# Feed-forward: both parts of an activation in one 512-column product, the down projection in two passes

## Chip, cores and metric

The kernel runs on one core of a Trainium2 chip. The metric is the device time of one execution in microseconds: 1619.3 us, the median of three runs from 1618.78 to 1620.37.

## What is computed

A transformer block with attention, a gated recurrence and 16 experts is followed by a second block of two layers. Each of these layers is a feed-forward, a mixer, and a second feed-forward, on 256 tokens of width 1024. The change touches the four feed-forwards (width 2816) and, in the layout of the activations only, every projection:

```python
def swiglu(x, w_gate, w_up, w_down):
    return (jax.nn.silu(x @ w_gate) * (x @ w_up)) @ w_down

for l in range(DEPTH_2):
    h = x + 0.5 * swiglu(rms_norm_2(x, ffn1_norm[l]), ffn1_gate[l], ffn1_up[l], ffn1_down[l])
    ...
    x = h + 0.5 * swiglu(rms_norm_2(h, ffn2_norm[l]), ffn2_gate[l], ffn2_up[l], ffn2_down[l])
return rms_norm_2(x, final_norm)
```

Everything is float32.

## The kernel before

Activations lie with features on partitions and the 256 tokens along the row; a matrix of 1024 features is eight chunks of 128. A float32 product is made of float32r ones: weights and activations are each split in a high part (a rounded copy, by ScalarE) and a low part (what is left, by VectorE). `mm3` (L409) multiplies low weights by high activations, high by low and high by high, three products of 256 columns into one region of PSUM, each with a weight load of its own.

Weights come in slots of 1 MB ([128, 2048]) through four raw buffers, in a fixed order (`stream`); `pump` fetches when a raw buffer is free. `cut` (L331) splits half a slot: ScalarE writes 128x1024 of `wh` (L333), VectorE the same of `wl` (L334). A split slot takes two of the 17 ring buffers of 8 KB; x, the norm's two parts and the mixer's large tiles live in the same ring. `ahead(i)` (L343) splits slot i and up to `la` further ones while the ring has room beyond `hold`, with a priority that lies `late` instructions behind. A scheduler orders each engine's instructions by priority as their operands become ready; on the chip each engine then runs its queue in that order. Splits traced after a norm's reciprocal root are kept behind it on VectorE (`gate`).

PSUM has eight banks: a pool of four (`pa`), one of three (`pb`) and one alone (`pc`).

A feed-forward (`ffn`, L1241) has 22 steps j. A gate/up slot holds 128 gate and 128 up columns; `proj` (L578) makes their 48 products into one bank, gate in one half and up in the other. `evac` (L1247) multiplies by the norm's row (VectorE, 512 columns), takes Silu of the gate (ScalarE), multiplies by up (VectorE) and splits the result in `hh` (ScalarE) and `hl` (VectorE). `down` (L1260) multiplies them with half a down slot, 24 products over all eight output chunks, which accumulate in the four banks of `pa` over all 22 steps, two chunks in a bank. Step j's down products come two steps later.

`start_phase` (L502) begins a phase: for each of eight chunks the residual's update from PSUM (VectorE, `adder`), the split of x times the norm's weight (ScalarE and VectorE), its square, and the products of the first three slots with this chunk. In the last chunk the sum of squares goes through TensorE (`fin1`), then come the reciprocal root on VectorE and its transposition (`fin2`), in the middle of the next projection. The first feed-forward starts beside the last expert with one slot (`first_phase`). After the last feed-forward the final norm runs with no weights left to multiply.

Of the kernel before, what the change touches and what calls it, by code (L numbers as in the profile page):

```python
# [140 lines left out]
def _prepare(i):  # L141
# [14 lines left out]
    for l in range(2):  # L156
        for n in ("ffn1", "ffn2"):
            ga, up = _pairs(f[n + "_gate_2"][l], st), _pairs(f[n + "_up_2"][l], st)
            out[f"{n}gu{l}"] = np.stack([ga, up], axis=3).reshape(NF, 128, 2048)
            out[f"{n}d{l}"] = _rows(f[n + "_down_2"][l])  # L160
# [49 lines left out]
# ---------------------------------------------------------------- the kernel  # L210
# [11 lines left out]
def _body(tc, nc, const, ringp, work, psum, a, out):  # L222
    V, S, PE, G = nc.vector, nc.scalar, nc.tensor, nc.gpsimd

    # ------------------------------------------------------------ memory
    st = {"ring": 0, "raw": 0, "next": 0, "hold": 0, "la": 2, "late": 0, "gate": None}
# [11 lines left out]
    def later(n):  # L238
        """as if traced n instructions further on"""
# [37 lines left out]
    # the first slot of block 2 is split while the last one of the experts is on its way  # L277
# [86 lines left out]
    def keep_warm(n, w, x, late=5000):  # L364
        """n products that nobody reads, for gaps in which TensorE's clock would fall back"""
# [5 lines left out]
    # ------------------------------------------------------------ constants  # L371
# [37 lines left out]
    def mm3(ps, wh, wl, xh, xl, first, last):  # L409
        PE.matmul(ps, lhsT=wl, rhs=xh, start=first, stop=False, skip_group_check=True)  # L410
        PE.matmul(ps, lhsT=wh, rhs=xl, start=False, stop=False, skip_group_check=True)  # L411
        PE.matmul(ps, lhsT=wh, rhs=xh, start=False, stop=last, skip_group_check=True)  # L412

    def behind(i, j):
        """i is issued after j, both on one engine"""
# [3 lines left out]
    def hilo(hi, lo, src):  # L419
        """src (SBUF or PSUM) in two float32r parts"""  # L420
# [3 lines left out]
    class Norm:  # L424
        """x * g in parts, and 1/rms of x: by tokens on partitions (rt) and along rows (rb)."""

        def __init__(self, g, parts=True, late=0):
# [3 lines left out]
            if parts:  # L431
                self.xh = ralloc([128, 8, 256], F32R, "xh")
                self.xl = ralloc([128, 8, 256], F32R, "xl")
# [3 lines left out]
        def split(self, c):  # L437
                xc = xt[:, c]
                g = self.g[:, c:c + 1]
                h = S.activation(self.xh[:, c], xc, AF.Copy, scale=g)  # L440
                l = V.scalar_tensor_tensor(self.xl[:, c], xc, g, self.xh[:, c].bitcast(F32),
                                       op0=OP.mult, op1=OP.subtract)
# [7 lines left out]
        def square(self, c, add=True):  # L450
            """add: into the sum; else left to TensorE"""
# [20 lines left out]
        def fin2(self, rev=False, bank=pc):  # L472
            """rev: also the rows with each 128 tokens back to front (rr)"""
# [16 lines left out]
    def wpair(i):  # L490
        """slot of two output chunks -> (hi, lo) by (chunk, contraction chunk)"""
# [4 lines left out]
    def warm(func):  # L496
        """the table of func, ahead of its use"""
# [3 lines left out]
    def start_phase(norm, update, jobs, each=None, bank=None, func=None):  # L501
        """Chunk by chunk: the residual's update, its parts, and the first products.  # L502
        jobs: (output, weights by chunk, first of its bank, last of its bank)"""
        for c in range(8):
# [6 lines left out]
            for n, (ps, w, first, last) in enumerate(jobs):  # L511
# [3 lines left out]
                mm3(ps, wh, wl, norm.xh[:, c], norm.xl[:, c], c == 0 and first, c == 7 and last)  # L515

    def ordered(*seq):
        """issued in this order, all on one engine"""
# [3 lines left out]
    def first_phase(norm, update, i, ps, each):  # L522
        """start_phase for one slot, step by step beside the last expert"""
# [34 lines left out]
        for c in range(8):  # L558
            each(c)
            for m in range(2):  # L560
                if c == 7 and m:
                    norm.fin1(pa)
                mm3(ps[:, m], wh[:, m, c], wl[:, m, c], norm.xh[:, c], norm.xl[:, c],
                    c == 0 and m == 0, c == 7 and m == 1)
# [10 lines left out]
    def proj(norm, i, ps, mid=None):  # L575
        ahead(i)
        wh, wl = wpair(i)
        for m in range(2):  # L578
            for c in range(8):
                mm3(ps[:, m], wh[:, m, c], wl[:, m, c], norm.xh[:, c], norm.xl[:, c], c == 0, c == 7)  # L580
# [4 lines left out]
    def proj_t(norm, i, ps, mid=None):  # L585
        """512 output columns with tokens on partitions; ps: a bank for each 128 tokens"""
        for s in range(2):
# [4 lines left out]
            for t in range(2):  # L592
                for k in range(4):
                    c = 4 * s + k
                    xh, xl = (x[:, c, 128 * t:128 * t + 128] for x in (norm.xh, norm.xl))
# [8 lines left out]
    def out_proj(slots, order, mh, ml, each=None):  # L604
        """contraction chunks in the order of the slots, all 8 output chunks at a time"""
        acc = [pa(f"acc{b}") for b in range(4)]
        for n, i in enumerate(slots):
# [3 lines left out]
            def mul(m, o):  # L611
                k = order[2 * n + m]
                f, z = n == 0 and m == 0, n == len(slots) - 1 and m == 1
                mm3(acc[o // 2][:, o % 2], wh[:, m, o], wl[:, m, o], mh[:, k], ml[:, k],
# [23 lines left out]

    def run(gen, n=1):
# [5 lines left out]
    # ================================================================ block 1  # L645
# [31 lines left out]
    # lower bounds of the forget gates: softmax over the two rows, the first of them  # L677
# [24 lines left out]
    def gates(p, d, h):  # L702
        """heads h, h + 1 of direction d: f -> T0, k -> AL (forward) or AR (backward)"""
# [39 lines left out]
    def hgrn():  # L743
        """A[s, t] of every head: what each token t takes of each token s, level by level"""
# [821 lines left out]
```

## Time and profile before

| | |
|---|---|
| median of three runs | 1619.3 us (1618.78, 1619.3, 1620.37) |
| span of the profiled execution, first to last instruction | 1618.6 us; no other time is listed for it |
| instructions | 28848 |
| TensorE, VectorE, ScalarE busy | 1504.8, 821.7, 609.5 us |
| read from memory | 397.99 MB |

The page gives each engine's busy time, the span in 40 slices, the DMA queues, and a chain of waits followed back from the last instruction. From 0 to about 190 us the first mixer runs, then the experts, whose weights are read as they are, to about 640 us, and then the second block. PE is TensorE's products, PEld its weight loads, DVE VectorE, ACT ScalarE. A product's listed duration reaches from its start to the end of its results, so consecutive ones overlap; the distance between two starts is the pace.

### The profile page before, as it was taken

The page shows a single profiled execution, that of the slowest core. Times are in us where ns is not written, and L with a number is a line of the kernel's source. Part 1 is how long each engine was busy: PE and PEld are TensorE (multiplying, and loading weights), DVE is VectorE, ACT ScalarE, POOL GpSimd, SP SyncE. Part 2 cuts the span into 40 slices and gives each one's busy share as a digit, 9 for nine tenths or more (in the row PEclk, how much of TensorE's full clock was granted, in tenths as well). Part 3 has the DMA queues.
Part 4 walks back from the last instruction along what each step waited for, and adds up shares of the span by engine and source line. Part 5 has one row for each costly group of instructions (what it writes and reads, how often), then busy time and mean ns, then how long its engine had stood idle before and what let it go on. Part 6 is the DMA issues. An engine that isn't in the chain of part 4 may idle for free.

```text
span 1618.6 us, 28848 instructions
## 1 busy us (share of the span) xinstructions
PE 1504.8 (93%) x12440; PEld 1265.0 (78%) x12440; DVE 821.7 (51%) x1472; ACT 609.5 (38%) x992; POOL 6.1 (0%) x11
## 2 busy tenths in 40 slices
PE   9999988777686779999999999999999999999998
PEld 9887633222232236999999999999999999999997
DVE  7975412000000003955548866655755648866653
ACT  6445201000000002644446655444443437655432
POOL 0000000000000000000000000000000000000000
PEclk9999999777878769999999999999999999999999
DMA  7546799999999998855433637453555433637520
GB/s 298 187 153 240 305 403 421 421 420 421 421 421 421 421 422 347 294 204 186 176 124 107 254 117 292 161 204 131 208 208 184 159 122 131 247 114 277 182 79 27
DMA packets 59167, 400.90 MB, mean 248 GB/s; under 512 B 6560, under 2 KB 9760, under 8 KB 11424
## 3 DMA queue, kind: packets, MB, share of 16 engines
q1 hardware_dynamic: 58896, 398.93, 64.0%
q8 instruction: 97, 1.59, 0.4%
q14 instruction: 30, 0.25, 0.0%
q10 hardware_dynamic: 144, 0.14, 0.0%
HBM read 397.99 MB, written 1.05 MB: 247 GB/s over the span
## 4 chain that ended last, share of the span: by engine, by line
PE 78%; DMA 16%; DVE 3%; ACT 1%; issue 1%; DVEq 0%; SPq 0%; ACTq 0%
DMA w<-in_we 16%; PE gu L410 10%; PE gu L412 10%; PE gu L411 10%; PE dn L410 5%; PE dn L412 5%; PE dn L411 5%; PE y L1223 3%; PE gu L1180 3%; PE moe L1208 3%; PE acc L411 1%; PE acc L410 1%; PE acc L412 1%; PE qk L410 1%; PE qk L411 1%; PE qk L412 1%
## 5 line engine op out<-in xcount | busy, mean ns | idle before, releaser
L333 ACT ACTIVATE wh<-w 128x1024 fp32r<-128x1024 f32 (+1 forms) x365 | 368.4, 1048 | 292.1 <-PE gu L410 247.1
L334 DVE TENSOR_TENSOR wl<-w,wh 128x1024 fp32r<-128x1024 f32 (+1 forms) x365 | 433.6, 1217 | 24.2 <-ACT wh L333 23.7
L410 PE MATMUL gu<-xh,wl 128*128 128x256 f32 x1408 | 398.8, 283 | 0.1
L412 PE MATMUL gu<-xh,wh 128*128 128x256 f32 x1408 | 398.6, 283 | 0.0
L411 PE MATMUL gu<-xl,wh 128*128 128x256 f32 x1408 | 398.4, 283 | 0.0
L410 PEld LDWEIGHTS gu<-xh,wl 128*128 128x128 f32 x1408 | 270.1, 192 | 0.7 <-PE rbT L477 0.4
L411 PEld LDWEIGHTS gu<-xl,wh 128*128 128x128 f32 x1408 | 270.3, 192 | 0.0
L412 PEld LDWEIGHTS gu<-xh,wh 128*128 128x128 f32 x1408 | 270.2, 192 | 0.0
L411 PE MATMUL dn<-hl,wh 128*128 128x256 f32 x704 | 197.7, 283 | 0.0
L412 PE MATMUL dn<-hh,wh 128*128 128x256 f32 x704 | 197.7, 283 | 0.0
L410 PE MATMUL dn<-hh,wl 128*128 128x256 f32 x704 | 195.9, 284 | 0.0
L1180 PE MATMUL gu<-w,xin 128*32 128x512 f32 x1024 | 136.4, 642 | 40.4 <-DMA w<-in_we 39.6
L1250 DVE TENSOR_TENSOR fz<-gu,rb 128x512 f32<-128x512 f32 x88 | 60.4, 689 | 213.1 <-PE gu L412 213.1
L412 PEld LDWEIGHTS dn<-hh,wh 128*128 128x128 f32 x704 | 134.9, 192 | 0.0
L411 PEld LDWEIGHTS dn<-hl,wh 128*128 128x128 f32 x704 | 134.9, 192 | 0.0
L410 PEld LDWEIGHTS dn<-hh,wl 128*128 128x128 f32 x704 | 133.3, 192 | 1.1 <-ACT hh L421 1.1
L1180 PEld LDWEIGHTS gu<-w,xin 128*32 128x32 f32 x1024 | 28.0, 112 | 123.3 <-DMA w<-in_we 78.8
L1208 PE MATMUL moe<-scat,ys 128*128 128x256 f32 x256 | 94.5, 505 | 28.5 <-DVE ys L1230 14.7
L1208 PEld LDWEIGHTS moe<-scat,ys 128*128 128x128 f32 x256 | 56.0, 242 | 77.7 <-ACT ys L1232 35.1
L1230 DVE COPY ys<-y 128x256 f32<-128x256 f32 x34 | 14.4, 424 | 196.5 <-PE y L1223 196.5
L1223 PE MATMUL y<-w,hidT 128*32 128x256 f32 x1024 | 97.4, 507 | 8.2 <-ACT hidT L1203 8.2
L1196 ACT ACTIVATE sg<-gu 64x512 f32<-64x512 f32 x16 | 9.4, 590 | 242.5 <-PE gu L1180 242.5
(383 smaller groups left out, 2034.5 us busy)
## 6 DMA issues: line engine op xcount, KB each, us to landing
w<-in_we SPq DMA_DIRECT2D x192, 1024.0 KB, 19.8
w<-in_ffn1gu SPq DMA_DIRECT2D x44, 1024.0 KB, 4.8
w<-in_ffn2gu SPq DMA_DIRECT2D x44, 1024.0 KB, 4.9
w<-in_ffn1d SPq DMA_DIRECT2D x22, 1024.0 KB, 4.8
w<-in_wm SPq DMA_DIRECT2D x22, 1024.0 KB, 4.8
w<-in_ffn2d SPq DMA_DIRECT2D x22, 1024.0 KB, 5.5
w<-in_w SPq DMA_DIRECT2D x14, 1024.0 KB, 5.5
w<-in_wo SPq DMA_DIRECT2D x8, 1024.0 KB, 4.8
```

The lines of the kernel that those rows point to most:

```text
L333: hi = S.activation(wh, raw[i][:, a0:a1], AF.Copy)
L334: lo = V.tensor_tensor(wl, raw[i][:, a0:a1], wh.bitcast(F32), op=OP.subtract)
L410: PE.matmul(ps, lhsT=wl, rhs=xh, start=first, stop=False, skip_group_check=True)
L411: PE.matmul(ps, lhsT=wh, rhs=xl, start=False, stop=False, skip_group_check=True)
L412: PE.matmul(ps, lhsT=wh, rhs=xh, start=False, stop=last, skip_group_check=True)
L1180: PE.matmul(pg[32 * g:32 * g + 32], lhsT=xin[k // 4][:, k % 4, 32 * e:32 * e + 32], rhs=w[:, g], start=k == 0, stop=k == 7, skip_group_che ...
L1196: S.activation(sg, pg[0:64], AF.Silu)
L1208: PE.matmul(macc[s][:, m], lhsT=ys[s][:, 128 * m:128 * m + 128], rhs=sc, start=e == 0 and m == 0, stop=e == NE - 1 and m == 1, skip_group_ ...
L1223: PE.matmul(p[32 * g:32 * g + 32], lhsT=hT[:, g, k // 4], rhs=w[:, k], start=k < 4, stop=k >= 4, skip_group_check=True, tile_position=(0, ...
L1230: st["ys"] = V.tensor_copy(ys[s], p)
L1250: V.tensor_tensor(z, p, norm.rb2, op=OP.mult)
```

## The change

`mm2` replaces `mm3` in the feed-forwards. An activation's low and high part now lie side by side ([.., 2, 256], low first; class `Parts` for the norm's and the mixers' activations, `hx` for the hidden ones). One product of 512 columns multiplies the high weights with both parts into a whole bank, low half and high half; one of 256 columns adds low weights times high part to the low half. The two halves are added when the bank is read: ScalarE copies the low half, VectorE adds the high half from PSUM. All other projections keep three products and only take their operands from the new layout.

An output chunk so takes a whole bank. A gate/up step has two banks, from `pb` with four (the third and fourth step's from `pa`); the down projection accumulates four of the eight output chunks beside the gate/up steps, three steps behind them (two of its steps in the first), and the other four in a second pass after the last step, from the hidden activations kept in six ring buffers. Down weights are laid out by halves of the output (`_halves`): five slots of four steps for each pass and one for the last two steps of both. The first pass's last step comes after the first four of the second pass, and its four residual updates follow it at once. A residual update is two VectorE instructions (`adder2`). `pc` now draws from `pb`, and after each feed-forward the two pools change names (`turn`). A feed-forward starts with two slots instead of three (the first one still with one), and `hold` reserves the six buffers from its beginning.

Comments and documentation strings are also gone. The diff's core:

```diff
+def _halves(w):
+    a = w.reshape(22, 128, 2, 512).transpose(2, 0, 1, 3)
+    four = lambda b: b.reshape(-1, 4, 128, 512).transpose(0, 2, 1, 3).reshape(-1, 128, 2048)
+    return np.concatenate([four(a[0, :20]), four(np.concatenate([a[0, 20:], a[1, 20:]])), four(a[1, :20])])
...
     def pa(name, shape=(128, 2, 256)):
-        return psum.tile(list(shape), F32, name=name, tag="A", bufs=4)
+        return psum.tile(list(shape), F32, name=name, tag="AB"[st["turn"]], bufs=4)
     def pb(name, shape=(128, 2, 256)):
-        return psum.tile(list(shape), F32, name=name, tag="B", bufs=3)
+        return psum.tile(list(shape), F32, name=name, tag="BA"[st["turn"]], bufs=4)
     def pc(name, shape=(128, 512)):
-        return psum.tile(list(shape), F32, name=name, tag="C", bufs=1)
+        return pb(name, shape)
...
         for j in range(len(gu), NF):
             gu += add(a[f"{n}gu{l}"][j:j + 1], 1, 1)
-            if j == 3 or j > 3 and j % 2 == 0:
+            if j in (4, 7, 11, 15, 19, 21):
                 k = len(dn)
                 dn += add(a[f"{n}d{l}"][k:k + 1], 1, 1)
-        dn += add(a[f"{n}d{l}"][10:11], 1, 1)
+        dn += add(a[f"{n}d{l}"][6:11], 5, 1)
...
+    def mm2(ps, wh, wl, x, first, last):
+        PE.matmul(ps, lhsT=wh, rhs=x, start=first, stop=False, skip_group_check=True)
+        PE.matmul(ps[:, 0], lhsT=wl, rhs=x[:, 1], start=False, stop=last, skip_group_check=True)
+    class Parts:
+        def __init__(self, name):
+            self.half = [ralloc([128, 4, 2, 256], F32R, name) for _ in range(2)]
+        def __getitem__(self, c):
+            return self.half[c // 4][:, c % 4]
...
+    def adder2(acc, scale):
+        def update(c):
+            if c in acc:
+                for k in range(2):
+                    V.scalar_tensor_tensor(xt[:, c], acc[c][:, k], scale, xt[:, c], op0=OP.mult, op1=OP.add)
+        return update
...
         def evac(j):
             p = ps.pop(j)
-            z, s = t2("fz"), t1("fs")
-            V.tensor_tensor(z, p, norm.rb2, op=OP.mult)
+            z, zl, s, h = t2("fz"), t2("fl"), t1("fs"), t1("fh")
+            for m in range(2):
+                S.activation(zl[:, m], p[m][:, 0], AF.Copy)
+                V.tensor_tensor(z[:, m], p[m][:, 1], zl[:, m], op=OP.add)
+            V.tensor_tensor(z, z, norm.rb2, op=OP.mult)
             S.activation(s, z[:, 0], AF.Silu)
-            h = t1("fh")
             V.tensor_tensor(h, s, z[:, 1], op=OP.mult)
...
+            if j % 4 == 0:
+                hx.append(ralloc([128, 4, 2, 256], F32R, "hx"))
+                st["hold"] -= 1
+            x = hx[j // 4][:, j % 4]
+            hilo(x[:, 1], x[:, 0], h)
+        def down(acc, half, j):
+            k = (j // 4 if half == 0 else 6 + j // 4) if j < 20 else 5
+            u = j % 4 if j < 20 else j - 20 + 2 * half
             i = dn[k]
             ahead(i)
...
+            for o in range(4):
+                mm2(acc[4 * half + o], wh[:, u, o], wl[:, u, o], hx[j // 4][:, j % 4], j == 0, j == (21 if half == 0 else 19))
+            if u == 3:
                 done(i)
-        m = 1 if first else 3
+        m = 1 if first else 2
+        st["hold"] = 6
...
         for j in range(4, NF):
-            if j >= NF - 5:
-                st["hold"], st["la"], st["late"] = 2, LA[1], LATE[1]
-            ps[j] = pb("gu")
-            proj(norm, gu[j], ps[j])
-            down(j - 2)
+            ps[j] = [pb("gu"), pb("gu")]
+            proj(norm, gu[j], ps[j], mm=mm2)
+            if j == 4:
+                acc.update((o, pa(f"dn{o}")) for o in range(4))
             evac(j)
+            for _ in range(2 if j == 4 else 1):
+                down(acc, 0, lag)
+                lag += 1
         norm.free()
-        down(NF - 2, NF - 1)
-        return adder(acc, 0.5)
+        st["hold"], st["la"], st["late"] = 2, LA[1], LATE[1]
+        while lag < NF - 1:
+            down(acc, 0, lag)
+            lag += 1
+        acc.update((4 + o, pb(f"dn{4 + o}")) for o in range(4))
+        for j in range(4):
+            down(acc, 1, j)
+        down(acc, 0, NF - 1)
+        add = adder2(dict(acc), 0.5)
+        for c in range(4):
+            add(c)
+        for j in range(NF - 2, NF):
+            down(acc, 1, j)
+        for j in range(4, NF - 2):
+            down(acc, 1, j)
+        rfree(6)
+        st["turn"] ^= 1
+        return adder2({c: acc[c] for c in range(4, 8)}, 0.5)
```

## Rows read from the trace of the kernel before

**Rows 1.** The page: busy us (share) xinstructions; the granted clock.

```profile
PE 1504.8 (93%) x12440; PEld 1265.0 (78%) x12440; DVE 821.7 (51%) x1472; ACT 609.5 (38%) x992; POOL 6.1 (0%) x11
...
PEclk9999999777878769999999999999999999999999
```

**Rows 2.** The page's chain that ended last, by engine.

```profile
PE 78%; DMA 16%; DVE 3%; ACT 1%; issue 1%; DVEq 0%; SPq 0%; ACTq 0%
```

**Rows 3.** Stretches: us; PE, PEld, DVE, ACT, POOL busy; clock; DMA; GB/s.

```profile
400.00:500.00 100.00, 73.33 (x512) 26.45 (x512) 7.79 (x21) 5.22 (x12) 0.00 (x0) 0.79 1.01 421
...
1000.00:1100.00 100.00, 100.00 (x836) 100.00 (x835) 55.88 (x70) 41.05 (x56) 0.00 (x0) 1.00 0.53 189
```

**Rows 4.** Waits of PEld from 640 us: total us, times, longest us.

```profile
PEld rbT L1544 <- issue: 2.0, 1, 2.0
PEld dn L410 <- ACT hh L421: 1.1, 6, 0.2
...
PEld gu L410 <- PE rbT L477: 0.4, 1, 0.4
```

**Rows 5.** PE timeline, feed-forward: start us, duration us, group; first and last.

```profile
719.78 0.28 PE L411 MATMUL gu<-xl,wh 128*128 128x256 f32 x1
...
722.90 0.28 PE L410 MATMUL gu<-xh,wl 128*128 128x256 f32 x1
```

**Rows 6.** PE timeline, transposed projection: first and last of 22.

```profile
95.44 0.39 PE L602 MATMUL av<-wh,xh 128*128 128x512 f32 x1
...
100.20 0.39 PE L602 MATMUL av<-wh,xh 128*128 128x512 f32 x1
```

**Rows 7.** PEld timeline at the last sum of squares (runs merged).

```profile
1607.53 0.19 PEld L412 LDWEIGHTS dn<-hh,wh 128*128 128x128 f32 x1
...
1608.11 1.87 PEld L464 LDWEIGHTS ssT<-cst,sq 128*128 128x128 f32 x16
```

**Rows 8.** Page, costliest groups: xcount | busy us, mean ns | idle before.

```profile
L410 PE MATMUL gu<-xh,wl 128*128 128x256 f32 x1408 | 398.8, 283 | 0.1
...
L410 PE MATMUL dn<-hh,wl 128*128 128x256 f32 x704 | 195.9, 284 | 0.0
```

**Rows 9.** Groups by line and shape, VectorE and ScalarE.

```profile
L334 DVE TENSOR_TENSOR wl<-w,wh 128x1024 fp32r<-128x1024 f32 x363 | 432.3, 1220 | 23.8 <-ACT wh L333 23.3
...
L333 ACT ACTIVATE wh<-w 128x1024 fp32r<-128x1024 f32 x363 | 367.2, 1050 | 291.8 <-PE gu L410 247.1 <-PE dn L410 15.9 <-DMA w<-in_ffn2gu 13.6
...
L1250 DVE TENSOR_TENSOR fz<-gu,rb 128x512 f32<-128x512 f32 x88 | 60.4, 689 | 213.1 <-PE gu L412 213.1
...
L422 DVE TENSOR_TENSOR hl<-fh,hh 128x256 fp32r<-128x256 f32 x88 | 37.0, 420 | 17.7 <-ACT hh L421 17.6
L1253 DVE TENSOR_TENSOR fh<-fs,fz 128x256 f32<-128x256 f32 x88 | 36.8, 418 | 2.1 <-ACT fs L1251 2.1
...
L1251 ACT ACTIVATE fs<-fz 128x256 f32<-128x256 f32 x88 | 35.6, 404 | 30.2 <-DVE fz L1250 30.2
...
L1232 ACT ACTIVATE ys<-y 128x256 f32<-128x256 f32 x30 | 11.5, 383 | 130.1 <-PE y L1223 130.1
...
L634 DVE TENSOR_TENSOR x<-acc,x 128x256 f32<-128x256 f32 x24 | 9.1, 418 | 13.2 <-PE acc L412 13.2
```

**Rows 10.** DVE timeline at a feed-forward's start [idle before].

```profile
950.25 0.16 DVE L469 TENSOR_SCALAR var<-ssT 128x2 f32<-128x2 f32 x1 [10.44 <-PE ssT L464]
...
951.90 3.49 DVE L334 TENSOR_TENSOR wl<-w,wh 128x1024 fp32r<-128x1024 f32 x3
...
974.26 2.35 DVE L334 TENSOR_TENSOR wl<-w,wh 128x1024 fp32r<-128x1024 f32 x2
```

**Rows 11.** Timeline at the end of the last feed-forward, all engines.

```profile
1607.47 1.25 DVE L636 SCALAR_TENSOR_TENSOR x<-dn,x 128x256 f32<-128x256 f32 x3
...
1607.65 0.28 PE L412 MATMUL dn<-hh,wh 128*128 128x256 f32 x1
```

**Rows 12.** Stretch at the end of the first mixer's output projection.

```profile
925.00:930.00 5.00, 5.00 (x44) 5.00 (x43) 1.66 (x3) 0.15 (x1) 0.00 (x0) 1.00 0.82 287
```

More of the change, by code (lines that the diff above doesn't have):

```diff
@@ L223, in _body @@
     V, S, PE, G = nc.vector, nc.scalar, nc.tensor, nc.gpsimd
-    st = {"ring": 0, "raw": 0, "next": 0, "hold": 0, "la": 2, "late": 0, "gate": None}
+    st = {"turn": 0, "ring": 0, "raw": 0, "next": 0, "hold": 0, "la": 2, "late": 0, "gate": None}
     def ralloc(shape, dt, name, tag="ring"):
@@ L407, in rsqrt, with mm3, lo, hi @@
             st["gate"] = last
[L409 to L412, printed above, removed]
+    def mm3(ps, wh, wl, x, first, last):
+        PE.matmul(ps, lhsT=wl, rhs=x[:, 1], start=first, stop=False, skip_group_check=True)
+        PE.matmul(ps, lhsT=wh, rhs=x[:, 0], start=False, stop=False, skip_group_check=True)
+        PE.matmul(ps, lhsT=wh, rhs=x[:, 1], start=False, stop=last, skip_group_check=True)
+    def mm2(ps, wh, wl, x, first, last):
[6 more added lines that the diff above has]
+            return self.half[c // 4][:, c % 4]
+        def lo(self, c, n=1):
+            return self.part(0, c, n)
+        def hi(self, c, n=1):
+            return self.part(1, c, n)
+        def part(self, k, c, n):
+            h = self.half[c // 4]
+            return h[:, c % 4, k] if n == 1 else h[:, c % 4:c % 4 + n, k]
     def behind(i, j):
@@ L499, in warm, with start_phase @@
         S.activation(w, xt[:, 7, 0:1], func)
-    def start_phase(norm, update, jobs, each=None, bank=None, func=None):
+    def start_phase(norm, update, jobs, each=None, bank=None, func=None, mm=mm3):
         for c in range(8):
@@ L514, in start_phase @@
                 wh, wl = w(c)
-                mm3(ps, wh, wl, norm.xh[:, c], norm.xl[:, c], c == 0 and first, c == 7 and last)
+                mm(ps, wh, wl, norm.x[c], c == 0 and first, c == 7 and last)
     def ordered(*seq):
@@ L562, in first_phase @@
                     norm.fin1(pa)
-                mm3(ps[:, m], wh[:, m, c], wl[:, m, c], norm.xh[:, c], norm.xl[:, c],
-                    c == 0 and m == 0, c == 7 and m == 1)
+                mm2(ps[m], wh[:, m, c], wl[:, m, c], norm.x[c], c == 0, c == 7)
         yield
@@ L573, in pair_jobs, with proj @@
         return jobs
-    def proj(norm, i, ps, mid=None):
+    def proj(norm, i, ps, mid=None, mm=mm3):
         ahead(i)
@@ L579, in proj @@
             for c in range(8):
-                mm3(ps[:, m], wh[:, m, c], wl[:, m, c], norm.xh[:, c], norm.xl[:, c], c == 0, c == 7)
+                mm(ps[m] if mm is mm2 else ps[:, m], wh[:, m, c], wl[:, m, c], norm.x[c], c == 0, c == 7)
                 if m == 0 and c == 7 and mid:
@@ L594, in proj_t @@
                     c = 4 * s + k
-                    xh, xl = (x[:, c, 128 * t:128 * t + 128] for x in (norm.xh, norm.xl))
+                    xl, xh = (norm.x[c][:, k_, 128 * t:128 * t + 128] for k_ in range(2))
                     mm3_t(ps[t], wh[:, k], wl[:, k], xh, xl, c == 0, c == 7)
@@ L602, in mm3_t, with out_proj @@
         PE.matmul(ps, lhsT=xh, rhs=wh, start=False, stop=last, skip_group_check=True)
-    def out_proj(slots, order, mh, ml, each=None):
+    def out_proj(slots, order, mx, each=None):
         acc = [pa(f"acc{b}") for b in range(4)]
@@ L1021, in _body @@
     run(ag, ATTN[3])
-    acc = out_proj(WO1, WO1_ORDER, mh, ml, lambda k: run(ag, ATTN[4]))
+    acc = out_proj(WO1, WO1_ORDER, mx, lambda k: run(ag, ATTN[4]))
     assert not run(ag)
@@ L1277, in ffn @@
             for j in range(m):
-                ps[j] = pb("gu")
+                ps[j] = [pb("gu"), pb("gu")]
                 split(gu[j])
-            start_phase(norm, update, pair_jobs(gu[0:m], [ps[j] for j in range(m)]), bank=pa, func=AF.Silu,
-                        each=lambda c: c == 5 and split(gu[m]))
+            jobs = []
+            for j in range(m):
+                wh, wl = wpair(gu[j])
+                for k in range(2):
+                    jobs.append((ps[j][k], lambda c, wh=wh, wl=wl, k=k: (wh[:, k, c], wl[:, k, c]), True, True))
@@ L1282, in ffn @@
+            start_phase(norm, update, jobs, bank=pa, func=AF.Silu, each=lambda c: c == 5 and split(gu[m]), mm=mm2)
         for j in range(m):
             done(gu[j])
-        st["hold"], st["la"], st["late"] = 0, LA[0], LATE[0]
-        for j in range(m, 3):
-            ps[j] = pb("gu")
-            proj(norm, gu[j], ps[j])
-        ps[3] = pc("gu", (128, 2, 256))
-        proj(norm, gu[3], ps[3], lambda: norm.fin2(bank=pa))
+        st["la"], st["late"] = LA[0], LATE[0]
+        for j in range(m, 4):
+            bank = pb if j < 2 else pa
+            ps[j] = [bank("gu"), bank("gu")]
+            proj(norm, gu[j], ps[j], (lambda: norm.fin2(bank=pa)) if j == m else None, mm=mm2)
@@ L1290, in ffn @@
         for j in range(4):
             evac(j)
-        down(0)
-        down(1)
+        acc, lag = {}, 0
         for j in range(4, NF):
-            if j >= NF - 5:
-                st["hold"], st["la"], st["late"] = 2, LA[1], LATE[1]
-            ps[j] = pb("gu")
-            proj(norm, gu[j], ps[j])
-            down(j - 2)
+            ps[j] = [pb("gu"), pb("gu")]
+            proj(norm, gu[j], ps[j], mm=mm2)
+            if j == 4:
+                acc.update((o, pa(f"dn{o}")) for o in range(4))
@@ L1522, in each @@
                 rfree()
-        acc = out_proj(WO[l], WO2_ORDER, mh, ml, each)
+        acc = out_proj(WO[l], WO2_ORDER, mx, each)
         rfree(2)
```

51 lines of the change are left out of this document (17 added, 34 removed).

## The prediction

> **What bounds the kernel now.** I read the page's busy line and clock line first: TensorE is busy 93% of a span of 1618.6 us, and its granted clock is 9 tenths or more everywhere but in the expert stretch [rows 1]. The chain of waits that ended last says the same by engine: PE 78%, DMA 16% [rows 2]. The table by stretch then splits the kernel in two. Between 400 and 500 us (experts) the DMA share is 1.01 at 421 GB/s and the clock 0.79: that stretch waits for weights and the change does not touch its transfers. Between 1000 and 1100 us (feed-forward) PE is busy 100.00 of 100 us at clock 1.00, the 2.4 GHz level, with VectorE at 55.88 and ScalarE at 41.05 [rows 3]. The list of waits of the weight loads from 640 us on has one entry of 2.0 us, in the final norm, and six more that sum to 3.2 us, two of them shown [rows 4]. So in the second block nothing is left to remove but TensorE's own pace, and only what shortens that pace, or newly stalls it, moves the time.
>
> **The pace.** In the PE timeline 27 products of 256 columns, feed-forward ones, start from 719.78 to 722.90 us: 26 steps of 120.0 ns [rows 5]. At 2.4 GHz 256 columns stream in 106.7 ns, so 13.3 ns of each step are something else. The transposed projection has 512-column products, each again with weights of its own: 22 starts from 95.44 to 100.20 us, 21 steps of 226.7 ns [rows 6]; 512 columns stream in 213.3 ns and the rest is 13.3 ns again. The rest belongs to the product, not to its columns. The other limit is the weight load. Sixteen loads for products of one column run for 1.87 us in all, and one load shows 0.19 us, so the loads follow each other at 1.68/15 = 112 ns [rows 7]. That is a floor which the 256-column product clears by 8 ns and the 512-column one by far.
>
> **The change part by part.**
>
> Products. A group is one weight chunk times both activation parts. Before: three products of 256 columns, 3 x 120.0 = 360.0 ns. After: one of 512 and one of 256, 226.7 + 120.0 = 346.7 ns. The columns are the same 768; what goes is one product's 13.3 ns and one load. There are 1408 groups for gate and up and 704 for down in the four feed-forwards [rows 8], 2112 x 13.3 ns = **-28.2 us**. The lower load count gives nothing more, since no load is exposed.
>
> The Trainium skill ("TensorE: Matmul & The Clock Gate", section "Back-to-back issue gap") puts a warm product at N/2.4 plus 2.5 ns. By that a group would go from 327.5 to 325.0 ns and the change would bring 2112 x 2.5 ns = 5.3 us. The trace differs: its fixed part is 13.3 ns at both widths.
>
> Evacuation. A gate/up pair now lies in two banks, low and high part side by side. Before, one pair cost VectorE 0.69 + 0.42 + 0.42 = 1.53 us and ScalarE 0.81 us (Silu 0.40, the high part taken as the same). After, it costs ScalarE two copies of 256 columns out of PSUM more, at 0.38 us each, and VectorE two adds from PSUM at 0.42 us each, while the multiplication stays at 0.69: VectorE 2.37, ScalarE 1.57 us [rows 9]. In the loop a step is 20 groups, 6.93 us of PE. It needs 1.25 slots split, a slot being two halves of 1.22 us on VectorE and 1.05 us on ScalarE: VectorE 3.05 + 2.37 = 5.42 us (78%), ScalarE 2.62 + 1.57 = 4.19 us (60%). Both stay below PE, so the loop hides them: 0. The next pair's banks are not waited for either, since four banks hold two pairs and a pair has the whole next step to be read.
>
> Lookahead. The hidden activations now keep six of the 17 ring buffers to the end of the second pass. With x (1), the norm's parts (2) and these, eight are left, four split slots, of which the current down slot keeps one for four steps. Counted through the code, the tightest places are steps 7, 11, 15 and 19 of each feed-forward: there the next gate/up slot may only be split when the slot two steps back is done, one step before its use. From release to use there are 6.9 us. One slot needs 1.05 us for the first high half, then 2.44 us on VectorE, and at worst one evacuation of 2.37 us ahead of it: 5.9 us. It fits by 1 us: 0, with the end of the range at the rival below.
>
> Start of a feed-forward. The first products now run for two slots instead of three: 32 groups, 11.1 us instead of 17.3 us. Splits traced after the norm's reciprocal root are held behind it. Before, VectorE sat idle 10.44 us for its sum, then had 1.7 us of small steps, and then worked without a gap until 976.6 us (974.26 + 2.35), while PE did not stop [rows 10]. After, from the end of the first products PE reaches the fourth slot at +5.5, the fifth at +11.1 and the down products at +16.6 us. VectorE has to do by then the rest of the root (1.6 us), three splits at 2.35 us a pair of halves (7.1 us) and four evacuations, back to back about 2.0 us each (7.9 us): 16.6 us. That is just even; the first two evacuations can start earlier only in their PSUM reads. Bounds: 0 if the order is good; 2.4 us, one split, if one slot comes late at each of the four starts. Nearer to the first, because the burst of before also cost nothing: 0.5 us each, **+2.0 us** (0 to 9.6). Nothing can be won here, as PE waited only 0.4 us at such a place [rows 4].
>
> Mixer. Before, two more of its slots were already split as the feed-forward ended; with four split slots in all one of them moves behind the gate, 2.4 us of VectorE each time. The out projection's end has slack: VectorE is busy 1.66 of 5 us at 925 to 930 us [rows 12]. I take 0 (0 to 4.8 for both mixers).
>
> Second pass and transitions. The down products are the same in number; its slots arrive one per 16 groups, 5.5 us, 1 MB each, 189 GB/s against the 421 GB/s of [rows 3]. Four of the eight residual updates now fall under the second pass. The other four, two VectorE instructions each, end behind it: eight at a pitch of 0.34 us, starting 1.04 us (three groups) before the last product ends, so 1.8 us past it. At three of the four ends the next phase's products for the first four chunks cover this (16 groups, 5.5 us, at least). At the last end nothing does. There, before, the last three updates ended at 1608.72, 0.8 us after the last product's end at 1607.93 [rows 11]: **+1.0 us** (0 to 2).
>
> Banks of one pool of four in place of three and one, and the new layout of the parts elsewhere: same products, same columns, same number of banks; 0, bounded by 1 us either way at the last expert, where the spare products and the two first banks share the pool.
>
> Sum against the profiled execution: 1618.6 - 28.2 + 2.0 + 1.0 = 1593.4 us. The median of the runs, 1619.3, is 0.7 us above that span, so **1594 us**, 1.6% less.
>
> **The rivals.**
>
> First, a part of the gain is given back at the starts and in the mixers. For it: the burst has no spare by my count. Against: before, the same burst ran without a stall. With a slot late at each start and the mixers' full bound, 9.6 - 2.0 + 4.8 = 12.4 us more: 1606.
>
> Second, the fixed part is not what I read, and the pair runs near three products' time, because the load of the next high weights can't hide under the 256-column product. For it: load and product differ by 8 ns there, hardly a reserve. Against: the 256-column stream runs exactly so, 26 times in a row [rows 5]. With no gain in the products it is 1619.3 + 3.0 = 1622: the change does not do what it says. By the page of the Trainium skill named above, gap and all, it would be 1617.
>
> Third, slower: the split slots come late. The place is the steps 7, 11, 15 and 19, 16 places in all. If splits stand behind both evacuation chains, each hopping between ScalarE and VectorE, a second slot's halves and all, PE waits there. The time before is reached at 25.2/16 = 1.6 us a place. A whole second split and a second evacuation in front, 4.8 us less the spare 1 us, cost 3.8 us a place, 61 us, so 1655. For it: TensorE has one step of lookahead there, where it had two to four. Against: averaged over the loop VectorE has 1.5 us free a step, and the order of before always put splits where they hid.
>
> **How the numbers follow.** Forecast (1588 to 1600): 0.75. First rival (1600 to 1612): 0.13. Second (1612 to 1623): 0.04, half of it beyond what can be told from no change. Third: 0.08. A measurement of this kernel can tell about 0.2%, 3.2 us. Faster: 0.75 + 0.13 + 0.01 = 0.89. Same: 0.02. Slower: 0.01 + 0.08 = 0.09. The range: at the lower end all stalls nothing and half of the 5.2 us of waits [rows 4] gone too, 1619.3 - 28.2 - 2.6 = 1588; at the upper end most of the first rival, 1607. It leaves out 0.09 above by the last two, 0.03 of the first and some 0.04 below.
>
> **What would show it.** Right: in the loop, starts 227 ns after a high product and 120 ns after a low one; PE still 100 of 100 us at clock 1.00, VectorE near 70 of 100; no TensorE wait for a split over 1 us; each feed-forward 7 us shorter. Wrong: a pair's steps sum to 360 ns, or waits of gate/up products for the low halves of the weights appear at the steps named, or the gap after the start phase grows.

## The result, and the profile after

The changed kernel takes 1604.8 us (median of four runs, 1602.9 to 1607.3), where the kernel before takes 1619.4 beside it: ratio 0.9911, 95% interval 0.9897 to 0.9925. It is faster, and inside the range that was given, but by 14.6 us and not by the 25.4 of the forecast. The span of its profiled execution is 1603.8 us (before: 1618.6). The forecast for that span was 1593.4, so 10.4 us have to be accounted for.

The page of the changed kernel (busy us, share, instructions; clock; chain; groups) answers to [rows 1, 2, 8, 9]:

```profile
PE 1478.1 (92%) x10328; PEld 1146.4 (71%) x10328; DVE 892.7 (56%) x1680; ACT 666.0 (42%) x1168; POOL 6.1 (0%) x11
...
PEclk9999999877877788999999999999999999999999
...
PE 69%; DMA 23%; DVE 5%; ACT 3%; issue 1%; DVEq 0%; SPq 0%; ACTq 0%
...
L425 PE MATMUL gu<-xs,wh 128*128 128x512 f32 x1408 | 494.7, 395 | 0.0
...
L426 PE MATMUL gu<-xs,wl 128*128 128x256 f32 x1408 | 392.0, 279 | 0.0
...
L1287 ACT ACTIVATE fl<-gu 128x256 f32<-128x256 f32 x176 | 65.9, 377 | 122.5 <-PE gu L426 122.1
L1288 DVE TENSOR_TENSOR fz<-gu,fl 128x256 f32<-128x256 f32 x176 | 73.8, 420 | 71.7 <-ACT fl L1287 71.3
```

The products changed as planned: 2112 fewer (12440 to 10328). TensorE is still the bound.

The next view, the table by stretch of the changed kernel, has two of the three places that matter (columns as in [rows 3]):

```profile
52.00:56.00 4.00, 1.93 (x194) 1.74 (x192) 4.00 (x5) 1.34 (x2) 0.00 (x0) 1.00 0.33 82
56.00:60.00 4.00, 2.04 (x67) 1.38 (x68) 4.00 (x7) 1.64 (x3) 0.00 (x0) 0.63 0.48 190
60.00:64.00 4.00, 4.00 (x18) 3.16 (x17) 4.00 (x6) 3.73 (x4) 0.00 (x0) 0.52 0.34 96
...
1000.00:1100.00 100.00, 100.00 (x579) 88.15 (x578) 75.68 (x114) 58.20 (x96) 0.00 (x0) 1.00 0.57 200
```

In the feed-forward (last line) PE is busy 100.00 of 100 us at clock 1.00, as before, with VectorE now at 75.68 in place of 55.88. Between 52 and 60 us, in the first mixer, PE is busy 3.97 of 8 us and the granted clock then falls to 0.63 and 0.52. The kernel before at the same place:

```profile
52.00:56.00 4.00, 4.00 (x212) 3.96 (x211) 4.00 (x6) 1.34 (x2) 0.00 (x0) 1.00 0.32 94
56.00:60.00 4.00, 4.00 (x33) 3.64 (x32) 4.00 (x7) 1.76 (x3) 0.00 (x0) 1.00 0.43 178
```

Laid side by side by the starts of the first and last TensorE products of each stage in the two profiled executions, the 14.8 us by which the spans differ come from here (worked out from the traces, us):

| stage | before | after | change | forecast |
|---|---|---|---|---|
| to the last expert's last product | 641.8 | 649.5 | **+7.7** | 0 |
| first feed-forward | 190.8 | 184.4 | -6.4 | |
| second | 191.2 | 183.9 | -7.3 | |
| third | 191.2 | 187.0 | **-4.2** | |
| fourth, to its last product's start | 190.8 | 183.8 | -7.0 | |
| the four together | 764.0 | 739.1 | -24.9 | -26.2 |
| the two later mixers | 201.8 | 203.2 | **+1.4** | 0 |
| from the last product's start to the end | 10.9 | 11.9 | +1.0 | +1.0 |

7.7 + 1.3 + 1.4 = 10.4 us. Three quarters of what is missing was lost before the first changed product ran: the first expert's first product starts at 197.07 us in place of 189.44, 7.6 us late already.

**Block 1.** The changed kernel's PE timeline there (start us, duration us, group, [idle before]):

```profile
53.21 0.71 PE L804 MATMUL lev<-AL,AR 128*32 128x32 f32 x62
57.81 1.08 PE L804 MATMUL lev<-AR,AL 128*32 128x32 f32 x64 [3.88 <-DVE AL L849]
59.05 1.89 PE L944 MATMUL pqk<-qsq,cst 128*16 128x256 f32 x4 [0.15 <-ACT qsq L941]
60.87 0.58 PE L418 MATMUL aqk<-xs,wl 128*128 128x256 f32 x1
61.25 0.41 PE L419 MATMUL aqk<-xs,wh 128*128 128x256 f32 x1
...
63.59 0.41 PE L418 MATMUL aqk<-xs,wl 128*128 128x256 f32 x1
```

The granted clock within that stretch, at its fall and at its rise (columns as in [rows 3]):

```profile
57.00:58.00 1.00, 0.19 (x13) 0.22 (x17) 1.00 (x2) 0.00 (x0) 0.00 (x0) 0.52 0.74 295
...
63.00:64.00 1.00, 1.00 (x7) 1.00 (x7) 1.00 (x2) 0.73 (x1) 0.00 (x0) 0.56 0.77 303
```

The kernel before there:

```profile
53.51 0.30 PE L766 MATMUL lev<-AL,AR 128*32 128x32 f32 x12
53.74 0.39 PE L410 MATMUL aqk<-xh,wl 128*128 128x256 f32 x1
...
59.57 1.04 PE L906 MATMUL pqk<-qsq,cst 128*16 128x256 f32 x4
```

Before, a whole projection (aqk, 48 products) follows a level of the HGRN recurrence (lev) and covers VectorE's work for the next level. After, the next level's products (57.81) and the sums of squares (pqk) stand ahead of that projection on TensorE. The level waits 3.88 us for VectorE, during which the granted clock falls to the 1.2 GHz level, and the projection starts at 60.87 in place of 53.74 us. Behind the idle time its first products run at that level: 11 steps from 61.25 to 63.59 us, 213 ns each, where 120 ns is the step at 2.4 GHz. Before, the last split of weights ahead of the projection, a low half on VectorE, ends at 53.48 us; the same one ends at 53.60 here, so the operands were there; it is the order that differs. By the first gate projection (hg, 87.03 in place of 80.04 us) 7.0 us are lost, 4.0 of them idle.

**The third feed-forward.** It has no stall. In the changed kernel's PE timeline, two unbroken runs of pairs of a 512- and a 256-column product, the first in the second feed-forward and the second in the third (first and last 512-column product of each):

```profile
955.15 0.39 PE L425 MATMUL gu<-xs,wh 128*128 128x512 f32 x1
...
1116.69 0.39 PE L425 MATMUL dn<-hx,wh 128*128 128x512 f32 x1
...
1146.40 0.40 PE L425 MATMUL gu<-xs,wh 128*128 128x512 f32 x1
...
1299.75 0.40 PE L425 MATMUL dn<-hx,wh 128*128 128x512 f32 x1
```

The first run has 466 pairs, 161.54 / 466 = 346.7 ns each, the number of the prediction. The second has 434, 153.35 / 434 = **353.3 ns**. Both at granted clock 1.00, both with PE always busy. Single steps in the first are 230 and 117 ns; in the second they go 236, 113, 233, 117, 241, 120 and round again, 1060 ns for three pairs.

### The profile page after: what moved, and what is told of

Its sections match the earlier page's. It is cut to its first block, busy times and chain, and to the rows that moved or that the text cites. A ratio compares the mean times of both kernels' runs of the same rounds, so it can differ in the third digit from the quotient of the medians.

```text
span 1603.8 us, 24974 instructions
## 1 busy us (share of the span) xinstructions
PE 1478.1 (92%) x10328; PEld 1146.4 (71%) x10328; DVE 892.7 (56%) x1680; ACT 666.0 (42%) x1168; POOL 6.1 (0%) x11
## 4 chain that ended last, share of the span: by engine, by line
PE 69%; DMA 23%; DVE 5%; ACT 3%; issue 1%; DVEq 0%; SPq 0%; ACTq 0%
DMA w<-in_we 22%; PE gu L425 20%; PE gu L426 10%; PE dn L425 10%; PE dn L426 5%; PE acc L419 1%; PE gu L1217 1%; PE acc L418 1%; PE acc L420 1%; PE y L1260 1%; DVE wl L342 1%; ACT wh L341 1%; PE moe L1245 1%; PE junk L377 1%; PE qk L420 1%
## 5 line engine op out<-in xcount | busy, mean ns | idle before, releaser
L425 PE MATMUL gu<-xs,wh 128*128 128x512 f32 x1408 | 494.7, 395 | 0.0
L426 PE MATMUL gu<-xs,wl 128*128 128x256 f32 x1408 | 392.0, 279 | 0.0
L425 PEld LDWEIGHTS gu<-xs,wh 128*128 128x128 f32 x1408 | 263.7, 188 | 60.7
L426 PEld LDWEIGHTS gu<-xs,wl 128*128 128x128 f32 x1408 | 265.3, 188 | 0.5
L425 PE MATMUL dn<-hx,wh 128*128 128x512 f32 x704 | 248.5, 394 | 0.0
L426 PE MATMUL dn<-hx,wl 128*128 128x256 f32 x704 | 196.2, 279 | 0.0
L425 PEld LDWEIGHTS dn<-hx,wh 128*128 128x128 f32 x704 | 132.0, 187 | 30.8
L426 PEld LDWEIGHTS dn<-hx,wl 128*128 128x128 f32 x704 | 132.6, 188 | 0.0
L1287 ACT ACTIVATE fl<-gu 128x256 f32<-128x256 f32 x176 | 65.9, 377 | 122.5 <-PE gu L426 122.1
L1288 DVE TENSOR_TENSOR fz<-gu,fl 128x256 f32<-128x256 f32 x176 | 73.8, 420 | 71.7 <-ACT fl L1287 71.3
```

Source lines behind the costliest of these rows:

```text
L425: PE.matmul(ps, lhsT=wh, rhs=x, start=first, stop=False, skip_group_check=True)
L426: PE.matmul(ps[:, 0], lhsT=wl, rhs=x[:, 1], start=False, stop=last, skip_group_check=True)
L1287: S.activation(zl[:, m], p[m][:, 0], AF.Copy)
L1288: V.tensor_tensor(z[:, m], p[m][:, 1], zl[:, m], op=OP.add)
```

## The experiments

Three theories for the missing time. Theory 1: merging the pools of three banks and one into one of four changed the order that the build gives TensorE in block 1. Theory 2: the new layout of the parts costs time there. Theory 3: what is missing is in the feed-forwards.

**Three pools again in block 1.**

```diff
+    def bank(k, name, shape):
+        if k == "B" and st["blk"] == 2:
+            k = "BBBC"[st["n"] % 4]
+            st["n"] += 1
+        return psum.tile(list(shape), F32, name=name, tag=k, bufs={"A": 4, "B": 3, "C": 1}[k])
...
     def pc(name, shape=(128, 512)):
-        return pb(name, shape)
+        return bank("C", name, shape) if st["blk"] == 1 else pb(name, shape)
...
                 f = GU["ffn1", 0]
+                st["blk"] = 2
```

> The changed kernel, but until the last expert PSUM is dealt as in the kernel before: pools of four, three and one bank, with the sums of squares of q and k (pqk) in the bank by itself; from the first feed-forward on the pools of three and one are drawn from in turn as one of four. Theory 1 (the merged pool made the build put the second aqk product group behind the next level of HGRN, and with that lost the 7.7 us until the last expert): 1597 us, 7 to 8 less than the changed kernel, ratio to before 0.986. Theory 2 (the parts laid out side by side cost the time in block 1): unchanged at 1605. Theory 3 (what is missing is in the feed-forwards): 1605.

Measured: 1594.9 us, ratio 0.9851 (0.9838 to 0.9863). Theory 1 had 1597. In the profile 6.4 us are back by the first expert's first product (190.65 in place of 197.07), and 3.5 more come in the experts (see the end). The last expert's last product starts at 639.6 us, and the feed-forwards are as in the changed kernel (the third again 187.0). The stretch in block 1 is as before the change:

```profile
52.00:56.00 4.00, 4.00 (x211) 3.83 (x211) 4.00 (x6) 1.33 (x2) 0.00 (x0) 1.00 0.20 25
56.00:60.00 4.00, 4.00 (x36) 4.00 (x35) 4.00 (x7) 0.47 (x1) 0.00 (x0) 1.00 0.64 246
```

**The pools merged, nothing else.** The other direction, on the kernel before.

```diff
-        return psum.tile(list(shape), F32, name=name, tag="B", bufs=3)
+        return psum.tile(list(shape), F32, name=name, tag="B", bufs=4)
...
-        return psum.tile(list(shape), F32, name=name, tag="C", bufs=1)
+        return psum.tile(list(shape), F32, name=name, tag="B", bufs=4)
```

> The kernel before with one edit: the pools of three banks and of one become one pool of four. All products, layouts and weights as before. Theory 1: 1626 us, 6 to 8 slower, with the second aqk group behind pqk and a granted clock under 1 between 56 and 64 us. Theory 2 and theory 3: 1619, no change.

Measured: 1627.35 us, ratio 1.0054 (1.0042 to 1.0066), 8.6 us slower, a little more than expected. The same stretch of this kernel:

```profile
52.00:56.00 4.00, 2.70 (x200) 2.45 (x198) 4.00 (x7) 1.33 (x2) 0.00 (x0) 1.00 0.24 35
56.00:60.00 4.00, 0.94 (x65) 0.80 (x66) 4.00 (x6) 0.87 (x2) 0.00 (x0) 0.92 0.58 236
60.00:64.00 4.00, 4.00 (x15) 2.67 (x14) 4.00 (x5) 4.00 (x5) 0.00 (x0) 0.50 0.19 35
```

No product, weight or layout of it differs from before. So the pools alone make the loss, both ways. Of the 8.9 us by which the spans differ, 6.8 stand at the last expert (8.9 at the first expert's first product, 198.33 in place of 189.44 us; the experts then took 2.1 less) and 2.1 come in its first feed-forward, which the changed kernel doesn't show; that part was not followed.

**Which tile does it.** The changed kernel with its two pools of four; only pqk is drawn from the other one.

```diff
-    pqk = pc("pqk")
+    pqk = pa("pqk", (128, 512))
```

> The changed kernel with one word changed: the sums of squares pqk are drawn from the pool that HGRN's levels use and not from the one that the aqk groups use. Both pools keep four banks. If the loss comes from pqk and aqk sharing a pool (and not from the number of banks or from other tiles that moved to it): the second aqk group stands ahead of the next level again, 6 to 7 us come back, 1597 to 1598.5 us; the 1.5 us lost in the router stay, so 1 to 2 above the run with three pools. If the number of banks is what matters, or the other tiles: 1605.

Measured: 1599.3 us, ratio 0.9883 (0.9866 to 0.9900): 5.5 us come back by the medians, 4.5 by the ratios, where 6 to 7 were expected. That is just above the range given, and 4.4 above the run with three pools where 1 to 2 were expected. Its PE timeline has the old order:

```profile
53.95 0.39 PE L418 MATMUL aqk<-xs,wl 128*128 128x256 f32 x1
...
59.77 1.04 PE L944 MATMUL pqk<-qsq,cst 128*16 128x256 f32 x4
```

So with every other tile left where it was, taking pqk out of the pool of the aqk groups undoes the swap, and the number of banks is not the cause. Of the 4.4 us that lie between the spans of this kernel and of the one with three pools, 1.5 are in the router, which picks the tokens of each expert: from the first logits to the turned logits (lgT) it takes 6.8 us here and in the changed kernel, 5.2 before and with three pools (all 16 transposes hT ahead of lgT, before only four). The logits, lgT and the products `junk` beside them still share one pool here, but no run moved one of them alone. Another 1.5 us are in the experts, 0.8 in the tail, where the granted clock fell to 0.51, and the rest in the second block. Why the build places a group differently when two tiles share a pool was not settled.

**The layout of the parts, nothing else.** The kernel before, with the norm's and the mixers' parts side by side.

```diff
-                self.xh = ralloc([128, 8, 256], F32R, "xh")
-                self.xl = ralloc([128, 8, 256], F32R, "xl")
+                self.x = Parts("xs")
...
-                mm3(ps, wh, wl, norm.xh[:, c], norm.xl[:, c], c == 0 and first, c == 7 and last)
+                mm3(ps, wh, wl, norm.x[c], c == 0 and first, c == 7 and last)
```

> The kernel before with one edit: the low and high parts of an activation lie side by side, four chunks to a tile, in place of one tile for each part; three products a group, pools and weights as before. Theory 2 (the layout costs time in block 1): up to 8 us slower. Theory 1: the first mixer and the router as before, at most 1.5 us in all from the two later mixers, where the changed kernel took 101.5 us in place of 100.8 each: 1619 to 1620.5. If those 0.7 us too come from elsewhere: 1619 and mixers of 100.8.

Measured: 1620.2 us, ratio 1.0006 (0.9997 to 1.0015), which alone can't be told from no change. In the trace the two later mixers take 101.6 us each in place of 100.9, as in the changed kernel, and the logits come 0.2 us earlier than before. The layout explains the mixers' 1.4 us and nothing of block 1; what in the layout costs the mixers 0.7 us each was not followed. Theory 2 falls.

**Three products again.** As with three pools, but the 512-column product split.

```diff
-        PE.matmul(ps, lhsT=wh, rhs=x, start=first, stop=False, skip_group_check=True)
+        PE.matmul(ps[:, 0], lhsT=wh, rhs=x[:, 0], start=first, stop=False, skip_group_check=True)
+        PE.matmul(ps[:, 1], lhsT=wh, rhs=x[:, 1], start=False, stop=False, skip_group_check=True)
```

> As the run with three pools in block 1, but each 512-column product is two 256-column products again, with the same weights loaded for each, into the two halves of the same bank; evacuation, layouts and the two passes of the down projection stay. If the gain is the 13.3 ns that a group of three products spends above a 512- and a 256-column product, 2112 groups give back 28 us: 28 over the run with three pools, about 1625 (ratio 1.004). If part of the gain came from the two passes or from the other order of the weights, less comes back: under 20 us, below 1617.

Measured: 1618.65 us, ratio 1.0003 (0.9994 to 1.0011): 23.8 us over the run with three pools, between the two numbers expected. Steps are 120.0 ns in all four feed-forwards, but for a few near each start. PE timeline of this kernel, 13 steps:

```profile
1000.10 0.28 PE L432 MATMUL gu<-xs,wh 128*128 128x256 f32 x1
...
1001.66 0.28 PE L433 MATMUL gu<-xs,wl 128*128 128x256 f32 x1
```

The third feed-forward is not longer than its neighbours (190.9 us, the second 190.7). The feed-forwards together are 24.6 us longer than with three pools. That is 2112 x 13.3 = 28.2 less some 550 pairs at 353.3 that had gained only 6.7 ns, 3.7 us: 24.5. So the whole gain is the product that is gone; the two passes and the evacuation cost or gain under 1 us (763.3 us of feed-forwards here, 764.0 before). All the rest of the change but the merged pool stands in this kernel, and it is as fast as the kernel before.

**Gate and up alone.** As with three pools, but the down projection in one pass with three products.

```diff
-            for o in range(4):
-                mm2(acc[4 * half + o], wh[:, u, o], wl[:, u, o], hx[j // 4][:, j % 4], j == 0, j == (21 if half == 0 else 19))
+            for o in range(8):
+                for j in js:
+                    mm3(acc[o // 2][:, o % 2], wh[:, j % 2, o], wl[:, j % 2, o], hx[j // 4][:, j % 4],
+                        j == 0 and o % 2 == 0, j == NF - 1 and o % 2 == 1)
```

> As the run with three pools, but only the gate and up products (1408 groups) use 512 columns; the down projection is back to one pass over four banks with three 256-column products for each of its 704 groups, and its weights in the layout of before. If both halves of the change pay by their number of groups: 9.4 us over the run with three pools, some 1606. If the two passes with their longer lag cost something, less than that or nothing: 1597 to 1602. If the gate and up evacuation is what holds the rest back, more than 1608.

Measured: 1609.2 us, ratio 0.9943 (0.9930 to 0.9955): 14.3 over the run with three pools, not 9.4, and 9.5 below the kernel before, not 18.8. The PE timeline of this kernel, 16 pairs between two down steps:

```profile
1001.34 0.40 PE L431 MATMUL gu<-xs,wh 128*128 128x512 f32 x1
...
1006.64 0.40 PE L431 MATMUL gu<-xs,wh 128*128 128x512 f32 x1
```

5.30 / 15 = 353.3 ns. In all four feed-forwards the blocks of pairs that come between blocks of three products run at the slow step (means of 352.8 ns). 1408 x 6.7 = 9.4 us is what remains then, and what was measured. So the slow rhythm is no matter of the third feed-forward's place; here it comes after every block of 256-column products.

**Extra products.** As with three pools; in the third and fourth feed-forward a product that nobody reads ahead of steps 6, 9, 12, 15 and 18, of 64, 128, 192, 256 and 32 columns.

```diff
+                PE.matmul(ps[j][0][:, 0, :NUDGE[n, l][j]], lhsT=wpair(gu[j])[0][:, 0, 0],
+                          rhs=norm.x[0][:, 1, :NUDGE[n, l][j]], start=True, stop=False, skip_group_check=True)
             proj(norm, gu[j], ps[j], mm=mm2)
```

> As the run with three pools, but the third and the fourth feed-forward have one more product, that nobody reads, ahead of the gate and up products of steps 6, 9, 12, 15 and 18, of 64, 128, 192, 256 and 32 columns. In the changed kernel a pair (512 and 256 columns) takes 346.7 ns in three feed-forwards and 353.3 ns in the third, from its eighth microsecond or so to its end. If these are two steady rhythms of one stream, and what interrupts it chooses between them: the pitch of the pairs changes at some of the extra products, from 353.3 to 346.7 or back, and keeps its new value until the next one. If the third feed-forward is slow by where its operands lie: 353.3 throughout in the third and 346.7 in the fourth. The time is within 4 us of the run with three pools.

Measured once: 1598.0 us. The PE timeline around the first two extra products (L1346) of the third feed-forward, with the first and last 512-column product of the unbroken run between each:

```profile
1140.21 0.40 PE L433 MATMUL dn<-hx,wh 128*128 128x512 f32 x1
...
1148.69 0.40 PE L433 MATMUL dn<-hx,wh 128*128 128x512 f32 x1
...
1149.40 0.20 PE L1346 MATMUL gu<-xs,wh 128*128 128x64 f32 x1
...
1150.21 0.39 PE L433 MATMUL gu<-xs,wh 128*128 128x512 f32 x1
...
1169.97 0.39 PE L433 MATMUL dn<-hx,wh 128*128 128x512 f32 x1
...
1170.32 0.22 PE L1346 MATMUL gu<-xs,wh 128*128 128x128 f32 x1
...
1171.14 0.40 PE L433 MATMUL gu<-xs,wh 128*128 128x512 f32 x1
...
1190.93 0.40 PE L433 MATMUL dn<-hx,wh 128*128 128x512 f32 x1
```

24 pairs at 353.3, then 57 at 346.7, then 56 at 353.4 ns. The first extra product turned the slow rhythm into the fast one, the second turned it back, and between them it held. The last three left it slow. In the fourth feed-forward, fast to begin with, the five gave slow, fast, slow, fast, fast. So there are two steady rhythms; an interruption can choose, and the width alone doesn't say which.

**One extra product, to use it.** As with three pools, and the 64 columns ahead of step 6 of the third feed-forward alone; beside it the kernel with three pools again.

```diff
+    NUDGE = {("ffn1", 1): {6: 64}}
```

> The run with three pools with one extra product of 64 columns, that nobody reads, ahead of step 6 of the third feed-forward: the one that turned the pitch there from 353.3 to 346.7 ns when five such products were tried. If the pitch then stays, 142 us of pairs at 353.3 ns become 139.3: 2.7 us less in that feed-forward (184.3 us in place of 187.0), and 1592.2 us in all where the run with three pools has 1594.9. If an extra product merely shifts chance: 187 again, and 1595.

> The kernel of the run with three pools once more, to be compared with the one extra product on the same chip: 1594.9 us, the third feed-forward again at 353.3 ns a pair and 187.0 us long by either theory of the block 1; if the rhythm were chance from one execution to the next, another feed-forward, or none, would be the slow one.

Measured: 1591.8 us, ratio 0.9829 (0.9816 to 0.9842), beside 1596.05, ratio 0.9860 (0.9845 to 0.9874). The two intervals just miss each other, so the times alone would be thin; the traces settle it. The third feed-forward is 184.3 us long with the extra product and 187.0 without, the other stages agree within 0.7 us, and the repeated kernel is slow in the same feed-forward as the first time. PE timeline with the extra product, one unbroken run:

```profile
1160.03 0.39 PE L433 MATMUL dn<-hx,wh 128*128 128x512 f32 x1
...
1289.68 0.39 PE L433 MATMUL dn<-hx,wh 128*128 128x512 f32 x1
```

374 pairs at 346.7 ns. The repeated kernel without it, also unbroken, there:

```profile
1136.24 0.40 PE L431 MATMUL gu<-xs,wh 128*128 128x512 f32 x1
...
1295.95 0.40 PE L431 MATMUL dn<-hx,wh 128*128 128x512 f32 x1
```

452 pairs, 353.3 ns. The version with the extra product, 1.7% under the kernel before and some 13 us under the changed one, is the fastest of the study.

## Why the prediction was right and where it was wrong

**Products, -28.2: right in kind, -24.6 in size.** The step per product of 13.3 ns, read from two rows of widths that never followed each other, holds in the fast rhythm to the tenth of a nanosecond. The rule of the Trainium skill that stood against it, N/2.4 + 2.5 ns for one warm product ("TensorE: Matmul & The Clock Gate", "Back-to-back issue gap"), would give an estimated 325.0 ns a pair; the trace has 346.7 or 353.3. What the rows could not show is the second rhythm, because one width alone had only one step. Counted by its pairs, it took 3.2 us of the third feed-forward and 0.2 at the start of the second and of the fourth.

**Starts, +2.0: nothing at three of four.** With 2112 / 4 x 13.3 = 7.0 us a feed-forward, the second and fourth gained 7.3 and 7.0, and the third gained 4.2, which with the 3.2 of its slow pairs is 7.4. The burst of splits and evacuations, which I counted as just even, was hidden there. The first, which starts beside the last expert, gained 6.4; where its 0.6 went was not followed.

**Evacuation and lookahead, 0: right.** The copies took 0.377 and the adds 0.420 us, as taken from other rows. In the list of waits of the weight loads from 640 us, which answers to [rows 4], no gate, up or down product appears; its longest entries are the final norm's and the mixers':

```profile
PEld rbT L1600 <- issue: 2.0, 1, 2.0
PEld po L1492 <- ACT pT L1490: 1.4, 4, 0.5
```

**Mixers, 0 (0 to 4.8): 1.4**, and not by a slot behind the gate but by the layout of the parts, as the run with that alone shows.

**Tail, +1.0: right**, mechanism and size (two other runs have a tail 0.6 and 0.8 us longer, at a granted clock of 0.5). The changed kernel's timeline, which answers to [rows 11]:

```profile
1591.16 2.76 DVE L674 SCALAR_TENSOR_TENSOR x<-dn,x 128x256 f32<-128x256 f32 x8 [18.92 <-PE dn L426]
...
1591.88 0.28 PE L426 MATMUL dn<-hx,wl 128*128 128x256 f32 x1
```

Eight updates end at 1593.92, 1.8 us past the last product's end.

**The step that failed: "Banks of one pool of four in place of three and one, and the new layout of the parts elsewhere: same products, same columns, same number of banks; 0, bounded by 1 us either way at the last expert".** It cost 7.7 us for the banks, 8.6 where the merged pool stood alone, and, through the layout, the mixers' 1.4. I counted what the instructions do and how many banks there are, and looked for trouble only where the feed-forward begins. But the order on TensorE isn't in the source; the build derives it, and as the runs with the merged pool alone and with pqk elsewhere show, the pools enter into it. With two pools merged it put a short group that waits ahead of a long one that was ready, in a stage that the change doesn't mention.

**The rivals.** The time came out at the first rival's 1606, but not by its road: starts cost nothing at three of four, mixers a third of their bound. The second is refuted at 360 ns a pair, though the slow rhythm is half of it. The third (late slots) did not occur: PE is busy 100.00 of 100 us. None of them named the pools, so the chances were spread over the wrong places and the range held by its width: that it held is luck in part. Of the chances that the range leaves out above, the second and third rival hold 0.04 + 0.08 = 0.12, not the 0.09 given.

## What to carry to other kernels

A change of buffer pools can be a change of order wherever those pools are used. Before costing it at nothing, compare the engines' instruction orders in every stage that draws from them, or give long-lived tiles a pool of their own. When a stretch is 100% busy, its pitch can still be off: compare the pitch of the same pair of instructions in each repetition of a loop.

## What was unexpected in the hardware

A stream of alternating 512- and 256-column products, each with weights of its own, has two steady rhythms, 346.7 and 353.3 ns a pair (1.9%), at the same granted clock and with the engine never idle. It keeps the one that it has over more than 400 pairs and can change it when other products come between. In the second to fourth feed-forward the four profiles with the same products there (the changed kernel, pqk elsewhere, three pools twice) take the same rhythm at the same places. The first, which follows the experts, is not so regular: its pairs at 652 to 656 us take 352.6 ns in one profile of the three-pool kernel and 347.1 in the other. Streams of 256 columns alone show 120.0 ns only. What inside the engine decides was not found. And after the idle stretch of 4 us in block 1, products ran at half the clock for some 6 us (57.81 to 63.8), so that the stage lost 7.0 us where TensorE was idle for 4.0.

Left open: the experts, whose stretch waits for weights. From their first product to their last it takes 452.4 us before and 452.5 in the changed kernel, but 449.0 and 450.0 in the two profiles of the three-pool kernel and between 449.4 and 451.5 in the others. So the time at the last expert in a profile holds up to 3 us that are not block 1's, and the three-pool run got back more than block 1 had lost. What sets this was not studied.
